# A streaming encoder layer on one core: full-width gate, sample and decay products, mLSTM's old part scaled on ScalarE, and a table of additions by tile name in the order pass

## The chip, the cores and the metric

The kernel runs on one core of one Trainium2 chip. The metric is the device time of one execution in microseconds (us), lower is better. TensorE (PE), VectorE (DVE), ScalarE (ACT), GpSimd (POOL) and SyncE (SP, which here issues the DMA transfers) each run one list of instructions in the order in which it was written and wait for each other with semaphores.

## What is computed

One layer of a streaming encoder, on 1024 new prompt frames (no history) and 32 frames of a running stream with state, model width 1024:

```python
h, st = mixer(rms_norm(x, g_mix_pre), st, ...)
x = x + rms_norm(h, g_mix_post)
h, ffn_buf = conv_ffn(rms_norm(x, g_ffn_pre), ...)
x = x + rms_norm(h, g_ffn_post)

def mixer(xn, ...):
    gq, gk, gv, gg, gr, hq, hf, hi, hg, mq, mk, mv, mi, mf, mo = split(xn @ w_in)
    # GLA: 6 heads 32x64, log_a = log_sigmoid(gg @ gla_w_gate + b) / 16   (gg has 16 columns)
    # HGRN2: 5 heads 64x64, gate from hf
    #   both: S_t = diag(a_t) S_{t-1} + k_t v_t^T, o_t = S_t^T q_t
    # mLSTM: 5 heads 64x64, gates mi and mf (5 columns each), causal conv on q and k
    #   m_i = max(g, max_j dlog);  w = exp(dlog - m_i);  w0 = exp(g - m_i)
    #   num = (s * w) @ v + w0 * (q @ C);   den = sum(s * w) + w0 * (q @ n)
    cat = concat(head_norm(o) * gate(o) for the three groups)
    return cat @ w_out, states

def conv_ffn(xn, ...):
    gate, val = split(causal_dwconv(xn @ w_up, width 3))   # 2 x 2816 columns
    return (gelu(gate) * val) @ w_down
```

All is float32. The states and the last rows of the convolutions are outputs too.

## The kernel before, in words

**Precision.** A product of float32 matrices runs as three passes over high and low halves (`mm3`, lines 88 to 91; `split` makes the halves: a cast on ScalarE, line 95, and a subtraction, line 98). Names with h and l at the end are these halves, with r the raw weights.

**Units and groups.** The 1056 frames are nine units u: eight of 128 prompt frames and u = 8 with the 32 sample frames (DEC). Three groups g of units are projected together: 384, 384 and 256 + 32 columns. `xh`, `xl` hold a group's normalized frames by features (line 309 transposes, 311 and 312 split).

**Projection in.** Features-by-frames products `pf` (13 blocks, `feat`) feed q, k and gates. Frames-by-features products give the values v and output gates: for groups 0 and 1 `vg(blk)` (line 420) makes them directly in `pv`, for each unit with its own `xh` columns as the fixed operand; so for u = 8 that operand is 32 columns wide. Group 2 runs blocks 1 to 7 in `vg_across` (line 432): products `pv` by features for all 288 columns, ScalarE copies them to `vf` (line 450), and `back` transposes each unit into `pb` (line 438). `vg_store` (line 403) passes a result on (ScalarE copy, or a tanh and a VectorE product) and stores it to `v_d` and `g_d`. A weight's raw half is loaded at line 321; in groups 1 and 2 its low half comes back from `lt_d` (line 325), where group 0 stored it.

**Gates.** Block 0 also holds 26 gate columns (16 for GLA, 5 and 5 for mLSTM). They are copied to `tgs` (line 428), and three small products a unit with the identity (line 473) bring them onto partitions 64 to 79, 96 to 100 and 32 to 36 of `tg`; ScalarE copies them to `r_fm` and `r_ig` (474 to 476). `z0` and `z3` (529, 604) are GLA's gate products from the 16 rows; `rows` (533) scans mLSTM's gates, spreads chunk decays by `dcp` (582) and transposes per-frame scales into `cols` (588, tile of the `mi` ring).

**Mixer.** `mixer(u)` (line 674) works through chunks with many small products (32 or 64 rows and columns): transposed keys `kt` and `kw` (762 to 802), state updates `up`, outputs `og` and `oh` (line 776), scores by levels, `oi` (queries by old mLSTM state) and `om`. Lines 936 to 940 join mLSTM's parts: `hn` is `oi` times w0 from `cols` (two VectorE products over 3 and 2 heads of 65 columns), then `om` is added. `sd` (960) are the diagonal scores. It runs beside the projections of later groups.

**The rest.** `outproj` (1009), FFN up with seven block products `puw` to `puz` of a fast matrix multiplication (1145 to 1310), down likewise (`down_all`, 1312; `wd` its weights). `T1h`, `B22h` and such are halves of sums of blocks.

**What sets the order.** `order` (line 2013) takes the finished program, builds a graph of dependencies with a cost for each instruction, and simulates all five engines (`play`): each takes, of what is ready in the simulation, the instruction with the largest priority. The result is fixed as the order of each engine. The priority is the longest path to the end in ns, plus an addition from the table `AHEAD`: the first key with which the name of the instruction's first output tile begins counts, otherwise the key of its pool.

```python
name.startswith(k)), pool))                                     # 1808: first key of AHEAD, or the pool
return [t + AHEAD.get(p, 0) for t, p in zip(tail, self.pool)]   # 1856
```

For TensorE `choose` stays in a tile mode while it can, and leaves full products for small ones only where the small work collected is `GATE` ns or more or has waited `PATIENCE` ns, and its priority is `CHANGE` ns ahead.

## Time and profile before

| | |
|---|---|
| three runs | 1331.88, 1327.99, 1328.19 us; median 1328.19 |
| profiled execution, its time | 1327.83 us |
| its span in the trace | 1326.0 us |
| mean granted TensorE clock | 0.993 |
| first matrix product / end of the last | 1.75 / 1318.3 us |
| FFN up and most of down | 645 to 1130 us |

One execution was profiled. The page lists busy time by engine and by group of instructions; the trace also answers by stretch of time, by wait and as a timeline. A group reads: line, engine, operation, output <- inputs, shapes, xcount, busy us, mean ns, idle before. In a wait, the engine and line that waited stand left of the arrow, what ended the wait right of it. A timeline row has start, duration, engine, line, operation, xcount and, in brackets, the idle time before it and what released it. `128*16` is a tile mode: rows and columns of the array that the fixed operand takes. Matrix products are pipelined, so that a product's duration is longer than the distance between two starts.

### The profile page before, as it was taken

The numbers are of one execution on the slowest core, as the hardware profiler recorded it, in microseconds if no ns is written. First come the engines' busy times: TensorE is split into PE (matmuls) and PEld (weight loads), VectorE is DVE, ScalarE is ACT, GpSimd is POOL, SyncE is SP. The second block draws the span as 40 slices with busy tenths as digits, with TensorE's granted clock in tenths as the row PEclk, the third lists the DMA queues.
The fourth block names the chain that finished last, engine by engine and source line by source line (L and its number), as shares of the span: only waits on it lengthen the run. The fifth ranks groups of instructions, "written<-read, shape, count | busy, mean of one in ns | idle before, by whom it ended". The sixth has DMA issues, their size and how long they took to land. (4 is left out here: it accounts for less than half of the span.)

```text
span 1326.0 us, 30530 instructions
## 1 busy us (share of the span) xinstructions
PE 1293.3 (98%) x12005; PEld 1208.7 (91%) x12005; DVE 1034.2 (78%) x1877; ACT 724.8 (55%) x1432; POOL 181.1 (14%) x331
## 2 busy tenths in 40 slices
PE   8999999999998999999999999999999999999997
PEld 7999999999898888778899999999999999888886
DVE  6795559748788478779899998888888878676686
ACT  6555566546576454436754545445454455365664
POOL 2020001111011112223112211111111110010010
PEclk9999999999999999999999999999999999999999
DMA  9899879977899863545256643222232268887774
GB/s 333 283 337 334 268 264 317 318 252 247 279 317 297 307 234 116 176 119 157 104 191 195 217 153 121 95 99 81 90 121 97 97 217 286 295 273 259 226 251 179
DMA packets 148455, 285.25 MB, mean 215 GB/s; under 512 B 30071, under 2 KB 84503, under 8 KB 148311
## 3 DMA queue, kind: packets, MB, share of 16 engines
q1 hardware_dynamic: 148311, 283.30, 63.7%
q8 instruction: 94, 1.54, 0.5%
q14 instruction: 50, 0.41, 0.1%
HBM read 201.90 MB, written 81.34 MB: 214 GB/s over the span
## 5 line engine op out<-in xcount | busy, mean ns | idle before, releaser
L1257 DVE SCALAR_TENSOR_TENSOR y<-uu,fconv_sb,y 128x1060 f32<-128x1060 f32 x88 | 116.0, 1321 | 7.7 <-ACT y L1255 6.7
L98 DVE TENSOR_TENSOR hlp<-rp,hhp 128x384 fp32r<-128x384 f32 x77 | 42.5, 555 | 35.3 <-PE pdw L91 11.3
L1255 ACT ACTIVATE y<-uu,fconv_sb 128x1060 f32<-128x1060 f32 x44 | 56.2, 1277 | 22.9 <-POOL uu L1252 17.1
L95 ACT CAST hhp<-rp 128x384 fp32r<-128x384 f32 x77 | 39.6, 515 | 49.0 <-PE pdx L90 18.2
L1203 ACT COPY c<-pux 128x274 f32<-128x274 f32 (+1 forms) x132 | 46.2, 380 | 27.1 <-PE pux L91 25.0
L933 POOL TENSOR_TENSOR hrs<-hss,mhalf 128x5 f32<-128x5 f32 (+3 forms) x27 | 36.1, 1340 | 163.8 <-DVE hss L932 162.8
L98 DVE TENSOR_TENSOR wdp<-rp,wdp 128x512 fp32r<-128x512 f32 x77 | 52.0, 688 | 3.7 <-ACT wdp L95 2.6
L89 PE MATMUL pv<-wt_0h,xh 128*128 128x256 f32 (+2 forms) x195 | 53.1, 294 | 1.4 <-ACT xh L311 0.6
L95 ACT CAST wdp<-rp 128x512 fp32r<-128x512 f32 x77 | 47.0, 621 | 10.1 <-PE pdx L91 3.4
L91 PE MATMUL pv<-wt_0h,xl 128*128 128x256 f32 (+2 forms) x195 | 50.6, 286 | 0.2 <-DVE xl L312 0.2
L90 PE MATMUL pv<-wt_0l,xh 128*128 128x256 f32 (+2 forms) x195 | 50.4, 284 | 0.2 <-DVE wt_0l L98 0.2
L91 PE MATMUL pv<-wt_1h,xl 128*128 128x256 f32 (+2 forms) x195 | 48.1, 287 | 0.0
L89 PE MATMUL pv<-wt_1h,xh 128*128 128x256 f32 (+2 forms) x195 | 47.2, 285 | 0.0
L90 PE MATMUL pv<-wt_1l,xh 128*128 128x256 f32 (+2 forms) x195 | 46.9, 285 | 0.0
L1252 POOL COPY uu<-fcache_sb 128x2 f32<-128x2 f32 x44 | 19.0, 431 | 185.8 <-DVE uu L1208 185.8
L91 PE MATMUL pdx<-wdp,hlp 128*128 128x512 f32 x132 | 43.2, 391 | 0.0
L90 PE MATMUL pdx<-wdp,hhp 128*128 128x512 f32 x132 | 43.0, 389 | 0.0
L89 PE MATMUL pdx<-wdp,hhp 128*128 128x512 f32 x132 | 42.7, 391 | 0.0
L1254 POOL COPY fhalo<-uu 128x2 f32<-128x2 f32 x44 | 35.7, 812 | 50.5 <-DVE uu L1208 49.9
L89 PEld LDWEIGHTS pv<-wt_0h,xh 128*128 128x128 f32 (+1 forms) x195 | 34.8, 187 | 2.8 <-ACT xh L311 0.9
L211 POOL TENSOR_SCALAR gss<-gss 128x1 f32<-128x1 f32 (+1 forms) x9 | 6.7, 747 | 216.6 <-ACT gjk L1331 132.5
L91 PEld LDWEIGHTS pv<-wt_0h,xl 128*128 128x128 f32 (+1 forms) x195 | 34.3, 187 | 1.0 <-issue 0.4
(1784 smaller groups left out, 5124.4 us busy)
## 6 DMA issues: line engine op xcount, KB each, us to landing
h_d<-y SPq DMA_DIRECT2D x22, 530.0 KB, 3.3
rp<-t_d SPq DMA_DIRECT2D x44, 256.0 KB, 3.9
wt_0r<-in_w_tok SPq DMA_DIRECT2D x21, 512.0 KB, 6.1
wt_1r<-in_w_tok SPq DMA_DIRECT2D x21, 512.0 KB, 5.5
...
```

The source lines that it names most:

```text
L89: pe.matmul(ps, lh[0], rh[0], start=first, stop=False, **kw)
L90: pe.matmul(ps, lh[0], rh[1], start=False, stop=False, **kw)
L91: return pe.matmul(ps, lh[1], rh[0], start=False, stop=last, **kw)
L95: act.copy(hi, src)
L98: (eng or pool).tensor_tensor(lo, src, hi.bitcast(F32), op=ALU.subtract)
L211: pool.tensor_scalar(out, ss, other, EPS, op0=ALU.add, op1=ALU.add)
L933: pool.tensor_tensor(rs[:n, h0:h0 + nh], ss[:n, h0:h0 + nh], mhalf[:n, :nh], op=ALU.pow)
L1203: act.copy(t, ps)
L1252: pool.tensor_copy(u[:, GAP_S:GAP_S + 2], fcache[:, j, :])
L1254: pool.tensor_copy(fhalo[:, j, :], u[:, NCOL - 2:NCOL])
L1255: act.activation(y, u, AF.Identity, scale=fconv[:, j, 2:3], bias=fconv[:, j, 3:4])
L1257: dve.scalar_tensor_tensor(y, uu[i][:, s:s + NCOL], fconv[:, j, s:s + 1], y, op0=ALU.mult, op1=ALU.add)
```

## The change

The diff has four parts.

1. **Full rows and columns.** The sample unit's products and transposes (`pv`, `pb`, `kw`, `sd`, `turned`) use a 128-column operand that ends with its 32 frames, so results stand on partitions 96 to 127. `tgs` becomes a 128-column tile, zeroed on GpSimd, filled by a ScalarE copy of 16 columns and a VectorE copy of 2 x 5, and a unit's three products into `tg` become one full transpose. `z0` and `z3` read 96 rows instead of 16 (the others are zero in the weights), `z3` writes 128 columns; `dcp` reads 128 rows. For u = 8 four transposes and two copies to `kt` become one and four. The host swaps the mi and mf columns and moves a bias.
2. **hn on ScalarE.** Two VectorE products a unit become five ScalarE copies with a scale.
3. **The table.** `AHEAD` gets some 480 keys with values from -10500 to 18000 ns; most name single tiles. The key `pt` (130000) goes; many mixer tiles that went by their pool's 10000 have a key of their own.
4. `GATE` goes from 300 to 500 and `PATIENCE` from 3000 to 4000.

```diff
 def vg_store(blk, u, off, n, ps):
+    r = slice(128 - n, 128)
-        act.copy(o[:n], ps[:n, :256])
-        sp.dma_start(v_d[t:t + n, 256 * blk:256 * blk + 256], o[:n])
+        act.copy(o[r], ps[r, :256])
+        sp.dma_start(v_d[t:t + n, 256 * blk:256 * blk + 256], o[r])
...
 # vg
-    mm3(ps[:n, :N], (xh[:, k, off:off + n], xl[:, k, off:off + n]), ws[k], k == 0, k == 7)
+    mm3(ps, (xh[:, k, off + n - 128:off + n], xl[:, k, off + n - 128:off + n]), ws[k], k == 0, k == 7)
-    act.copy(tgs[:n, i, :], ps[:n, 256:])
+    act.copy(tgs[:, i, 64:80], ps[:, 256:272])
+    dve.tensor_copy(tgs[:, i].rearrange("p (a b) -> p a b", b=64)[:, :, 32:37],
+                    ps[:, 272:282].rearrange("p (a b) -> p a b", b=5))
 # back
-    pe.transpose(ps[:n, 128 * e:128 * e + 128], fs[e][:, off:off + n], ident)
+    pe.transpose(ps[:, 128 * e:128 * e + 128], fs[e][:, off + n - 128:off + n], ident)
 # gates
-tgs = pf.tile([128, 3, 26], F32, tag="tgs", name=f"tgs{g}")
+tgs = pf.tile([128, 3, 128], F32, tag="q", name=f"tgs{g}", bufs=2)
+pool.memset(tgs, 0.0)
-    for (r0, c0, c1) in ((64, 0, 16), (96, 16, 21), (32, 21, 26)):
-        pe.matmul(gt_[r0:r0 + c1 - c0, off:off + n], tgs[:n, i, c0:c1], ident[:n, :n], start=True, stop=True)
-act.copy(gg[64:80], gt_[64:80, :T])
+    pe.transpose(gt_[:, off + n - 128:off + n], tgs[:, i], ident)
+act.copy(gg[:96], gt_[:96, :T])
-pe.matmul(z0[:, :T], wg[64:80, 0:128], gg[64:80, :], start=True, stop=True)
+pe.matmul(z0[:, :T], wg[:96, 0:128], gg[:96], start=True, stop=True)
-pe.matmul(z3[:64, :T], wg[64:80, 128:192], gg[64:80, :], start=True, stop=True)
+pe.matmul(z3[:, :T], wg[:96, 64:192], gg[:96], start=True, stop=True)
...
 # rows
+pool.memset(dc, 0.0)
-    pe.matmul(dcp[:, f, :ci], self_[R, 128 * f:128 * f + 128], dc[R, :ci], start=True, stop=True)
+    pe.matmul(dcp[:, f, :ci], self_[:, 128 * f:128 * f + 128], dc[:, :ci], start=True, stop=True)
-    pe.transpose(pt[:n, :], st[:, off:off + n], ident)
+    pe.transpose(pt, st[:, off + n - 128:off + n], ident)
...
 # mixer
+if u == 8:
+    kps = small(128)
+    pe.transpose(kps, khf, ident)
+    for f in range(4):
+        act.copy(kt[:n, 128 * f:128 * f + 128], kps[n * f:n * f + n])
-for f0 in (0, 2):
+for f0 in (0, 2) if u < 8 else ():
...
-for e in range(2):
-    dve.tensor_tensor(hn[:n, e::2], ois[e][:n, :3 - e],
-                      cols[:n, 32:37].unsqueeze(2)[:, e::2].broadcast_to([n, 3 - e, 65]), op=ALU.mult)
+for h in range(5):
+    act.activation(hn[:n, h], ois[h % 2][:n, h // 2], AF.Copy, scale=cols[:n, 32 + h:33 + h])
...
-AHEAD = {"mx": 10000., "psm": 10000., "pdx0": 1400., "pdx1": 700., "pdw0": 1400., "pdw1": 700., "pt": 130000.}
-GATE, PATIENCE = 300., 3000.
+AHEAD = {
+    "fconv_sb": 2000, "wt0_1_0r": -2500, "wt0_2_0l": 500, "wt0_2_1r": -1000, "wt0_3_0h": -1000, "wt0_3_0l": -3500, "wt0_4_0h":
...
+    500, "uu": -1500, "v2": 4000, "v4": 2500, "v6": 1000, "v7": -8000, "vf": 6000, "vg": -4000, "w2": 500, "wd": -9000, "wf":
...
+GATE, PATIENCE = 500.0, 4000.0
```

What it does to the order, on both built programs: TensorE issues 10081 products and transposes for 10102, and leaves full tiles for smaller ones 79 times for 106. Nearly every instruction moves by some places; three places follow. In the rows, `x2` and such count equal instructions in a row.

The first is TensorE in group 0, from the last gate product to `z0`. `pf_8` is the projection of block 8. Before:

```order
L89 MATMUL pf_8_376<-xh_185,wf_8h 128x384
L90 MATMUL pf_8_376<-xl_186,wf_8h 128x384
L91 MATMUL pf_8_376<-xh_185,wf_8l 128x384
L473 MATMUL tg_356<-ident,tgs_202 16x128
L473 MATMUL tg_356<-ident,tgs_202 5x128 x2
L529 MATMUL z_0_419<-r_fm_354,wg_sb 128x384
L89 MATMUL pf_6_433<-xh_185,wf_6h 128x384
```

With the change:

```order
L89 MATMUL pf_8_374<-xh_185,wf_8h 128x384
L476 MATMUL tg_360<-ident,tgs_202 128x128
L90 MATMUL pf_8_374<-xl_186,wf_8h 128x384
L91 MATMUL pf_8_374<-xh_185,wf_8l 128x384
...
L89 MATMUL pf_8_374<-xh_185,wf_8h 128x384
L90 MATMUL pf_8_374<-xl_186,wf_8h 128x384
L532 MATMUL z_0_417<-r_fm_358,wg_sb 128x384
L91 MATMUL pf_8_374<-xh_185,wf_8l 128x384
L89 MATMUL pf_6_431<-xh_185,wf_6h 128x384
```

`z_0` stood right behind the gate products and now stands 13 products of `pf_8` behind the gate transpose.

The second is TensorE in group 2, where the transposes of block 4 go back (`pb7_4`, `pb8_4`: units 7 and 8); `og5`, `oh5` are output products of unit 5, `sm80` and `sm81` scores of unit 8. Before:

```order
L91 MATMUL pv2_5_1_6621<-xh2_4321,wt2_5_1l_6583 128x288
L672 MATMUL mi_167<-ident_126,kh8_7017 32x128 x2
L438 MATMUL pb7_4_6647<-ident_126,vf4_6503 128x128 x2
L438 MATMUL pb8_4_6655<-ident_126,vf4_6503 32x128 x2
L776 MATMUL sm80_7027<-mqk8_6902 32x32 x3
L776 MATMUL sm81_7028<-mqk8_6902 32x32 x2
L89 MATMUL pv2_6_0_6676<-xh2_4321,wt2_6_0h_6665 128x288
```

With the change:

```order
L91 MATMUL pv2_5_1_6636<-xh2_4328,wt2_5_1l_6598 128x288
L785 MATMUL og5_5335<-v5_5077,P_184 64x64 x3
L785 MATMUL oh5_5336<-v5_5077,P_184 64x64
...
L785 MATMUL oh5_5336<-v5_5077,P_184 64x64
L592 MATMUL mi_167<-ident_126,r_st_2_5789 128x128
L441 MATMUL pb7_4_6662<-ident_126,vf4_6518 128x128 x2
L441 MATMUL pb8_4_6670<-ident_126,vf4_6518 128x128
L89 MATMUL pv2_6_0_6691<-xh2_4328,wt2_6_0h_6680 128x288
```

Twenty-two small products of unit 5, which stood further up, and a transpose now stand between block 5 and the transposes of block 4; the 32-row transposes of unit 8 are full ones, and its scores have gone elsewhere.

The third is SyncE in group 2, around the load of the second low half of block 2 (`wt2_2_1l`). Before:

```order
L325 DMA wt2_2_0l_6328<-lt_d_94 128x1024
L321 DMA wt2_3_1r_6414<-in_w_tok 128x1024
...
L373 DMA out_q_mc<-pc_2_6169 128x3
L321 DMA wt2_4_0r_6491<-in_w_tok 128x1024
L691 DMA v5_5064<-v_d_84 128x704
L325 DMA wt2_2_1l_6334<-lt_d_94 128x1024
L325 DMA wt2_3_0l_6411<-lt_d_94 128x1024
```

With the change:

```order
L325 DMA wt2_2_0l_6343<-lt_d_94 128x1024
L321 DMA wt2_3_1r_6429<-in_w_tok 128x1024
L373 DMA out_q_mc<-pc_2_6184 128x3
L374 DMA out_p_mc<-pc_2_6184 128x3
L325 DMA wt2_2_1l_6349<-lt_d_94 128x1024
L321 DMA wt2_4_0r_6506<-in_w_tok 128x1024
L325 DMA wt2_3_0l_6426<-lt_d_94 128x1024
L325 DMA wt2_3_1l_6432<-lt_d_94 128x1024
L695 DMA v5_5077<-v_d_84 128x704
```

The low half now stands ahead of the next raw weight and of unit 5's values; the store of a unit's result and loads of unit 5's keys and masks, which are not shown, stand further up than before. At the start of SyncE's list the gain row `gx` (512 KB) comes ahead of the first frames `x0`, which stood first.

More of the change, by code (lines that the diff above doesn't have):

```diff
@@ L411, in vg_store @@
             th = mx.tile([128, 256], F32, tag="vth", name=f"vth{u}_{blk}", bufs=1)
-            tanh(th[:n], ps[:n, :256], 0.5)
+            tanh(th[r], ps[r, :256], 0.5)
             ns = min(max(704 - c0, 0), 256)
             if ns:
-                dve.scalar_tensor_tensor(o[:n, :ns], th[:n, :ns], 1.0, ps[:n, :ns], op0=ALU.add, op1=ALU.mult)
+                dve.scalar_tensor_tensor(o[r, :ns], th[r, :ns], 1.0, ps[r, :ns], op0=ALU.add, op1=ALU.mult)
             if ns < 256:
-                dve.tensor_scalar(o[:n, ns:], th[:n, ns:], 1.0, None, op0=ALU.add)
-            sp.dma_start(g_d[t:t + n, c0:c0 + 256], o[:n])
+                dve.tensor_scalar(o[r, ns:], th[r, ns:], 1.0, None, op0=ALU.add)
+            sp.dma_start(g_d[t:t + n, c0:c0 + 256], o[r])
         def vg(blk):
@@ L587, in rows @@
                 pt = small(128)
-                pe.transpose(pt[:n, :], st[:, off:off + n], ident)
+                pe.transpose(pt, st[:, off + n - 128:off + n], ident)
                 cl = mx.tile([128, 128], F32, tag="cols", name=f"cols{u}", bufs=6)
-                act.copy(cl[:n], pt[:n])
+                act.copy(cl[:n], pt[128 - n:])
                 cols_of[u] = cl
@@ L603, in inproj @@
         z3 = psb.tile([128, 512], F32, tag="big", name=f"z3_{g}")
-        pe.matmul(z3[:64, :T], wg[64:80, 128:192], gg[64:80, :], start=True, stop=True)
+        pe.matmul(z3[:, :T], wg[:96, 64:192], gg[:96], start=True, stop=True)
         def fill3(fr):
-            act.activation(fr[:64], z3[:64, :T], AF.Identity, bias=vecs[:64, 3:4])
+            act.activation(fr[:64], z3[64:, :T], AF.Identity, bias=vecs[64:, 3:4])
             act.copy(fr[64:], ps3[64:, :T])
@@ L796, in mixer @@
             for f in range(2 if h0 == 0 else 1):
-                first(pe.transpose, kp[:n, 2 * f:2 * f + 2, :].rearrange("p h d -> p (h d)"),
-                      mk[:, f, :] if h0 == 0 else mq[:, 2, :], ident)
+                into = kp[:, 2 * f:2 * f + 2, :].rearrange("p h d -> p (h d)")
+                if u < 8:
+                    first(pe.transpose, into, mk[:, f, :] if h0 == 0 else mq[:, 2, :], ident)
+                else:
+                    first(pe.transpose, into, mqk[:, n * f:n * f + 128], ident)
+            kr = slice(0, 128) if u < 8 else slice(96, 128) if h0 == 0 else slice(64, 96)
             if h0:
                 kp = kp[:, 1:2]
-            dve.tensor_tensor(kw[:n, h0:h1], kp[:n, :h1 - h0],
+            dve.tensor_tensor(kw[:n, h0:h1], kp[kr, :h1 - h0],
                                        cols[:n, 96 + h0:96 + h1].unsqueeze(2).broadcast_to([n, h1 - h0, 64]), op=ALU.mult)
@@ L959, in mixer @@
         sd = small(11)
+        if u == 8:
+            dve.memset(z[:, 128:224], 0.0)
         for f in range(4):
-            first(pe.matmul, sd[:n], z[:, f * n:f * n + n], of_head[:, f, :], start=f == 0, stop=f == 3)
+            first(pe.matmul, sd, z[:, f * n:f * n + 128], of_head[:, f, :], start=f == 0, stop=f == 3)
         put(0, sd[:n].unsqueeze(2).broadcast_to([n, 11, cl]))
@@ L1404, in turned @@
                 for d in range(4):
-                    pe.transpose(pts[hf][:n, 128 * d:128 * d + 128], accs[4 * hf + d][:, off[u]:off[u] + n], ident)
+                    pe.transpose(pts[hf][:, 128 * d:128 * d + 128], accs[4 * hf + d][:, off[u]:off[u] + 128], ident)
             finish(u, n, [p[:n] for p in pts])
@@ L1605, in body @@
     p4s.close()
-CHANGE = 1500.
-BACKLOG = 2000.
-SLACK = {"PE": 1000.}
-AHEAD = {"mx": 10000., "psm": 10000., "pdx0": 1400., "pdx1": 700., "pdw0": 1400., "pdw1": 700., "pt": 130000.}
-GATE, PATIENCE = 300., 3000.
+CHANGE = 1500.0
+BACKLOG = 2000.0
+SLACK = {"PE": 1000.0}
+AHEAD = {
[58 rows of a table added]
+    2000, "jk4": 0, "jk5": 4000, "jk7": 2000, "lbt": 500, "oh7": -4000, "oml": 2000, "pdx": -2000, "psm": 10000, "pux": 500,
[8 rows of a table added]
+GATE, PATIENCE = 500.0, 4000.0
 ENGINES = ("PE", "DVE", "Activation", "Pool", "SP")
@@ L2038, in _layout @@
     w_tok = np.ascontiguousarray(wt[1:])
-    w_tok0 = np.hstack([wv[:, :256], gg, mf, mi]).reshape(8, 128, 282).transpose(1, 0, 2)
+    w_tok0 = np.hstack([wv[:, :256], gg, mi, mf]).reshape(8, 128, 282).transpose(1, 0, 2)
     w_out = np.asarray(i["w_out"])[0][of_plane].reshape(8, 128, 1024)
@@ L2046, in _layout @@
     vecs[:, 0] = bg[:128]
-    vecs[:64, 3] = bg[128:]
+    vecs[64:, 3] = bg[128:]
     lb = np.asarray(i["hgrn_lb"])[0]
```

64 rows, old and new, of the table AHEAD are left out of this document.

## The prediction

> **What bounds the kernel now.** I read the page's first part, then busy times by stage, the waits of TensorE, and the timelines around the waits that the change touches.
>
> ```profile
> span 1326.0 us, 30530 instructions
> PE 1293.3 (98%) x12005; PEld 1208.7 (91%) x12005; DVE 1034.2 (78%) x1877; ACT 724.8 (55%) x1432; POOL 181.1 (14%) x331
> ```
>
> TensorE is busy 98% of the span, so work on the other engines counts only where TensorE waits for it. The stage table says where it does (first column of each pair busy us, then count; the last three columns are granted clock, DMA share, GB/s).
>
> ```profile
> 0.00:50.00 50.00, 44.67 (x269) 40.74 (x270) 34.66 (x61) 27.64 (x50) 10.46 (x29) 1.00 0.92 329
> 300.00:400.00 100.00, 98.39 (x1545) 92.24 (x1544) 83.49 (x213) 67.18 (x152) 13.30 (x20) 0.98 0.86 282
> 400.00:500.00 100.00, 92.23 (x1097) 81.97 (x1096) 70.59 (x179) 55.35 (x134) 11.94 (x12) 0.98 0.83 275
> 500.00:600.00 100.00, 97.02 (x1267) 76.28 (x1267) 77.39 (x160) 47.03 (x112) 22.37 (x31) 0.98 0.47 142
> 600.00:645.00 45.00, 40.87 (x237) 35.42 (x236) 37.60 (x43) 32.45 (x67) 11.39 (x13) 0.97 0.40 122
> 645.00:1130.00 485.00, 485.00 (x3915) 485.00 (x3915) 422.70 (x641) 243.11 (x433) 74.94 (x176) 1.00 0.42 147
> 1130.00:1160.00 30.00, 28.33 (x192) 26.01 (x191) 21.66 (x39) 12.81 (x26) 0.00 (x0) 1.00 0.90 297
> ```
>
> From 645 to 1130 (the FFN) TensorE never stops at full clock: a new order can win nothing there, only lose. Idle TensorE time is 5.3 us in the first stage, 1.6, 7.8, 3.0 and 4.1 in the four from 300 to 645, 1.7 around 1145: 23.5 in all. The first stage's 5.3 is mostly the first loads. Four waits that bear on the change, from the list of TensorE's waits (us in total, times, longest):
>
> ```profile
> PE pv L91 <- DMA wt_1l<-lt_d: 1.8, 1, 1.8
> PE puw L89 <- ACT T1h L1133: 1.5, 1, 1.5
> PE pb L438 <- ACT vf L450: 1.0, 1, 1.0
> PE z L529 <- ACT r_fm L474: 0.7, 1, 0.7
> ```
>
> Beside waiting, TensorE loses time to a granted clock of half. Two of its four such stretches, each with the stretch ahead of it (the third number from the end is the clock):
>
> ```profile
> 448.20:451.60 3.40, 1.91 (x19) 1.35 (x20) 2.27 (x9) 3.15 (x9) 0.70 (x1) 1.00 0.94 307
> 451.60:455.00 3.40, 3.40 (x17) 3.38 (x16) 0.27 (x1) 0.00 (x0) 0.00 (x0) 0.50 1.02 387
> 536.90:540.30 3.40, 2.88 (x33) 2.50 (x33) 1.72 (x4) 3.34 (x10) 0.86 (x2) 1.00 0.62 176
> 540.30:543.70 3.40, 3.40 (x46) 2.61 (x41) 3.40 (x5) 1.97 (x6) 0.00 (x0) 0.50 0.13 17
> ```
>
> Each is 3.4 us long and costs half of it, 1.7 us; four cost 6.8. Both follow a stretch in which TensorE was not fully busy, but 2.88 of 3.40 was already too little.
>
> **(a) Fewer changes of tile mode.** In the built order TensorE switches between full products (128 rows and columns) and smaller tiles 149 times where it did 194 times, in 79 detours for 106. A detour of before, the gates of two units:
>
> ```profile
> 163.74 0.29 PE L91 MATMUL pv<-wt_2h,xl 128*128 128x282 f32 x1
> 163.96 0.61 PE L473 MATMUL tg<-ident,tgs 128*16 128x128 f32 x12
> 164.50 0.44 PE L89 MATMUL pf<-xh,wf_8h 128*128 128x384 f32 x1
> 164.78 0.33 PE L90 MATMUL pf<-xl,wf_8h 128*128 128x384 f32 x1
> 164.96 0.34 PE L91 MATMUL pf<-xh,wf_8l 128*128 128x384 f32 x1
> ```
>
> The start of tg comes 0.22 us after the product before it, where such products elsewhere in this stretch follow each other in 0.13; the product behind the detour holds the engine 0.28 us where the next holds it 0.18. So a switch costs about 0.1 us, and 45 fewer save 4.5. The bounds: −2 if more than half of the switches removed stood in time when TensorE waited anyway; −8 if what is narrow in the 27 detours is saved too (tg alone: 0.54 for a pair against two full transposes of at most 0.15 by the row further down, 0.1 a unit, 0.9 in nine units, and 0.1 more a detour for the rest).
>
> Widening the sample unit's products costs nothing in themselves:
>
> ```profile
> 326.24 0.30 PE L89 MATMUL pv<-wt_0h,xh 128*32 128x282 f32 x1
> 326.37 0.29 PE L90 MATMUL pv<-wt_0l,xh 128*32 128x282 f32 x1
> ```
>
> Products of 32 columns start 0.13 apart, as the full ones do. [...]
>
> **(b) The wait of z0, −0.7** (0 to −0.7). In group 0 of before, z0 comes right behind the last tg. Now 13 pf_8 products, 0.18 us each by the rows at 164.78 and 164.96, stand between them: 2.3 us over a wait of 0.7. The copy that z0 waits for reads 96 rows instead of 16, on partitions side by side, so it gets no longer.
>
> **(c) The low half of weight block 2, −0.9** (0 to −1.8).
>
> ```profile
> 400.26 0.38 SPq L321 DMA_DIRECT2D wt_0r<-in_w_tok  x1
> 401.25 0.32 SPq L691 DMA_DIRECT2D v<-v_d  x1
> 402.55 0.32 SPq L325 DMA_DIRECT2D wt_1l<-lt_d  x1
> 408.33 0.40 PE L91 MATMUL pv<-xh,wt_1l 128*128 128x288 f32 x1 [1.84 <-DMA wt_1l<-lt_d]
> ```
>
> The load is issued at 402.55 behind a weight (wt_0r) and a load of v, and its product waits 1.84. Now it stands ahead of both, 402.55 − 400.26 = 2.3 us earlier by these rows. But larger transfers (a 768 KB set of keys, masks, the store of a unit's result) now stand further up on the same queue, at a DMA share of 0.83: half of the wait is what I take.
>
> **(d) Transposes back in group 2, −1.9** (0 to −2.7).
>
> ```profile
> 447.31 1.03 ACT L327 CAST wt_0h<-wt_0r 128x1024 fp32r<-128x1024 f32 x1
> 448.24 0.38 ACT L450 COPY vf<-pv 128x288 f32<-128x288 f32 x1
> 448.68 0.44 PE L438 MATMUL pb<-ident,vf 128*128 128x128 f32 x2 [0.99 <-ACT vf L450]
> ```
>
> The copy vf stands behind a weight's cast of 1.03 us on ScalarE, and pb waits 0.99 for it. Now 22 small products of the mixer stand ahead of these transposes of block 4; they fill the wait: −1.0. The half-clock stretch from 451.6 has its cause here, in a stretch busy 1.91 of 3.40: filled by 1.0 it has 2.9, by the row at 536.9 still not surely enough, so half of its 1.7 is counted: −0.9. [...]
>
> **(e) The start, +1.0** (0 to +1.7).
>
> ```profile
> 0.72 0.40 SPq L144 DMA_DIRECT2D x<-in_xp  x1
> 1.17 0.42 SPq L155 DMA_DIRECT2D gx<-in_grows  x1
> 8.23 0.90 ACT L95 CAST wt_0h<-wt_0r 128x846 fp32r<-128x846 f32 x1 [2.33 <-DMA wt_0r<-in_w_tok]
> 9.67 0.40 PE L89 MATMUL pv<-wt_0h,xh 128*128 128x282 f32 x1 [0.64 <-ACT xh L311]
> ```
>
> The gain row gx (spread over 128 partitions, 512 KB) now is issued ahead of the first x. The chain to the first product at 9.67 goes from x by its norm and transposes to xh; x lands later by up to 512 KB at 329 GB/s = 1.6 us. The first weight only lands at 8.2, so part of it is hidden, but the first product waits for xh, not for the weight: +1.0.
>
> **(f) The FFN's start, 0.**
>
> ```profile
> 636.12 0.60 PE L1101 MATMUL fxt<-ident,z 128*128 128x128 f32 x4
> 638.75 1.23 DVE L1144 TENSOR_TENSOR xg<-xg 128x1024 f32<-128x1024 f32 x1
> 640.23 0.38 PE L89 MATMUL puw<-T1h,S_0h 128*128 128x256 f32 x1 [1.48 <-ACT T1h L1133]
> ```
>
> (Four transposes in 0.60 are the 0.15 used above.) T1h is cast ahead of B22h now, up to 1 us earlier; but its sum ends on VectorE at 639.98, and T1l and the next sums follow there at 1.2 us each, so the second product waits instead. Nothing is counted.
>
> **(g) mLSTM's old part on ScalarE, +0.5** (0 to +7.9).
>
> ```profile
> L938 DVE TENSOR_TENSOR hn<-oi,cols x18: 270/314/364, 171.9 to 570.4; 128x195 f32<-128x195 f32 x8, 128x130 f32<-128x130 f32 x8, 32x195 f32<-32x195 f32 x1, 32x130 f32<-32x130 f32 x1
> L1104 ACT ACTIVATE xg<-fxt,gcols_sb 128x128 f32<-128x128 f32 x24 | 7.2, 379 | 0.4 <-PE fxt L1101 0.4
> ```
>
> Two products of 0.314 on VectorE a unit (0.63) become five scaled copies. The nearest row, scaled copies of 128 columns out of PSUM, gives 7.2 / 24 = 0.30 each: 1.5, so hn comes up to 0.9 later, 7.9 in nine units. In the new order 14 to 113 TensorE products stand between the one that feeds hn and the next that needs its buffers, over 1.8 us at 0.13; only unit 8 has four. Half of one unit counts. VectorE gets 5.6 us back, which no TensorE wait of before asked for.
>
> The other edits cost 0: two more copies a unit into the gate tile, its three memsets and dc's on GpSimd (14% busy), and unit 8's two more ScalarE copies lie beside TensorE's products; if that cover is gone, each is 0.2 to 0.4 by the copy row at 448.24.
>
> **(h) All the rest of the order, −6.** The table moves nearly every instruction, and I can follow only a few places. What there is to win: 23.5 idle and 6.8 of half clock, 30.3, less 3.5 counted in (b), (c), (d): 26.8. At the places followed, waits of 5.0 us (z0, wt_1l, pb, puw) give back 2.6, and the start takes 1.0: net 1.6 of 5.0, a third. I take a quarter, since moved loads make new waits that no row shows: two loads for the down projection now stand behind more stores. Bounds: half of it, −13, and +8, the same waits growing by 30%.
>
> **Sum:** −4.5 −0.7 −0.9 −1.9 +1.0 +0 +0.5 −6 = −12.5. The profiled execution took 1327.83 (span 1326.0 and 1.8 around it), 0.36 below the median of 1328.19, so the two need no correction: 1315. Its own range, with (a) and (h) the widest terms, is 1306 to 1324.
>
> **The rivals.**
>
> *The order gives nothing (0.16).* Only (a), (e) and (g) hold, the waits come back elsewhere: −4.5 + 1.0 + 0.5 = −3.0, 1324.8. That is within 0.3% (4 us), about what a measurement of this kernel can tell from no change. For it: between 645 and 1130 nothing can be won. Against it: the waits of (b) and (d) visibly get cover.
>
> *The order gives far more (0.15).* If (h) takes 70% of the 26.8, −19: 1302. For it: the idle time lies in 300 to 645, where much small work is at hand to fill it. Against: (e) and (f).
>
> *ScalarE becomes the late engine (0.07).* If hn is waited for in every unit: −13.0 + 7.9 = −5.1, 1322.7. For it: in 448.2 to 451.6 ScalarE is busy 3.15 of 3.40. Against: 0.55 over the whole span.
>
> *Half clock spreads (0.11), the slower side.* The new settings gather small products longer (500 and 4000 ns for 300 and 3000) and release them in longer detours. At 536.9, 33 products, TensorE busy 2.88 of 3.40, and the clock halved for the next 3.4 us. If the longer detours of units 0 to 8 (130 to 600) each leave such a stretch, every one costs 1.7. Without (h) the sum is −6.5: four more stretches cancel it, from seven on it is slower by over 0.3%, and ten give −6.5 + 17 = +10.5, 1338. Against: fewer detours, and 100 to 300, full of small work, has clock 1.00.
>
> **How the numbers follow.** The forecast keeps 0.51. The range leaves out the tail of the large gain (under 1300) and that of the half clock (over 1331): 1300 to 1331. Faster by over 0.3%: forecast, large gain and late ScalarE, 0.51 + 0.15 + 0.07 = 0.73; the same: 0.16; slower: 0.11.
>
> **What would show it.** Right: tg's transposes without a gap of 0.1 around them, no wait of z0 and of pb for vf in the list of TensorE's waits, 400 to 500 with 94 or more busy, the first product near 10.7, puw still waiting about 1.5. Wrong: idle TensorE time between 645 and 1130, more than six stretches at clock 0.50, waits for hn or for a load of the down projection over 2 us, or a time over 1331 or under 1300.

## The result, and the profile after

| | before | with the change |
|---|---|---|
| runs, median | 1328.09 us (1324.92 to 1331.88, 4 runs) | 1311.62 us (1309.83 to 1314.21, 4 runs) |
| ratio | | 0.9875, 95% interval 0.9852 to 0.9899 |
| profiled execution, its time / span | 1327.83 / 1326.0 us | 1314.21 / 1312.4 us |

The change takes off 16.5 us by the medians and 13.6 by the profiled spans; the profiled execution of the changed kernel is the slowest of its four. 1315 was forecast, in a range of 1300 to 1331. A second measurement of the same kernel, among the experiments below, gave a ratio of 0.9897 (0.987 to 0.9924).

The page of the changed kernel begins so:

```profile
span 1312.4 us, 30429 instructions
PE 1285.7 (98%) x11957; PEld 1209.7 (92%) x11957; DVE 1024.5 (78%) x1869; ACT 728.5 (56%) x1479; POOL 169.6 (13%) x337
```

TensorE stands outside its busy time for 26.7 us of the span (1312.4 − 1285.7), where it was 32.7. The stages (same columns as before: stretch, busy us and count of TensorE, weight loads, VectorE, ScalarE, GpSimd, then granted clock, DMA share, GB/s):

```profile
0.00:50.00 50.00, 43.46 (x243) 41.74 (x244) 33.89 (x62) 27.21 (x49) 9.70 (x31) 0.93 0.93 323
100.00:200.00 100.00, 96.69 (x1043) 93.65 (x1042) 54.83 (x115) 55.49 (x112) 4.72 (x10) 1.00 0.85 295
300.00:400.00 100.00, 99.21 (x1591) 94.25 (x1591) 81.48 (x207) 67.83 (x162) 12.65 (x21) 1.00 0.86 289
400.00:500.00 100.00, 99.04 (x1272) 89.32 (x1272) 78.76 (x191) 65.45 (x162) 13.36 (x17) 1.00 0.83 287
500.00:600.00 100.00, 98.81 (x1184) 78.11 (x1183) 83.53 (x165) 52.08 (x130) 21.04 (x28) 1.00 0.48 151
600.00:645.00 45.00, 41.50 (x293) 38.36 (x292) 39.12 (x49) 32.16 (x63) 10.86 (x19) 1.00 0.37 125
645.00:1130.00 485.00, 483.92 (x3898) 483.46 (x3897) 410.45 (x636) 239.41 (x432) 68.17 (x168) 1.00 0.43 151
```

From 300 to 645 the idle time fell from 16.5 us to 6.4, and the clock is 1.00 throughout, where it was 0.97 to 0.98: 400 to 500, the worst stage of before, went from 92.23 busy to 99.04. The start got worse (5.3 idle to 6.5, clock 1.00 to 0.93). So did 100 to 200, which read in before:

```profile
100.00:200.00 100.00, 99.11 (x959) 94.85 (x959) 55.46 (x118) 56.53 (x111) 4.63 (x11) 1.00 0.85 288
```

The idle time there grew from 0.9 to 3.3 us; 1.2 of it is one wait of mi for kw, 1.3 one of pv for vg. From 645 to 1130, where TensorE never stopped before, it idles 1.1, in a wait of pd for hh; the second trace of the same kernel (experiment 5) has 485.00 busy there.

The longest waits of TensorE are mostly others now (us in total, times, longest; left out are one of 1.7 for the identity at the start, which both kernels have, and two of 1.0 and 0.8):

```profile
PE pv L89 <- ACT vg L408: 4.2, 4, 2.1
PE xt L309 <- DVE x L298: 2.6, 2, 1.6
PE pd L89 <- ACT wd L95: 1.8, 1, 1.8
PE mi L676 <- DVE kw L814: 1.2, 1, 1.2
PE puw L89 <- ACT T1h L1147: 0.8, 1, 0.8
```

The waits of pv for wt_1l (1.8), of pb for vf (1.0) and of z for r_fm (0.7) are gone from the list; puw waits 0.8 for 1.5. In their place stand pv for vg, the first transposes xt, and the last weight block wd of the first down stage. And the half-clock stretch at 451.6 is gone, with the emptier stretch ahead of it:

```profile
448.20:451.60 3.40, 3.40 (x28) 3.40 (x27) 3.37 (x15) 2.69 (x13) 1.16 (x1) 1.00 0.98 318
451.60:455.00 3.40, 3.40 (x60) 3.10 (x59) 3.21 (x10) 3.13 (x5) 0.00 (x0) 1.00 0.99 369
1137.20:1140.60 3.40, 1.63 (x13) 1.40 (x12) 0.75 (x2) 0.82 (x2) 0.00 (x0) 1.00 0.76 297
1140.70:1144.10 3.40, 3.40 (x16) 3.40 (x16) 2.71 (x6) 2.65 (x7) 0.00 (x0) 0.52 0.58 220
```

The third and fourth row are one of the three stretches that are left or new: the wait for wd leaves TensorE busy 1.63 of 3.40, and the next 3.4 us run at half clock. The other two lie in the first 30 us.

To see what kind of time went, I took from the traces the distance from each recorded product's start to the next, halved it where the clock was 0.50 (the half taken off is "half clock"), subtracted what such a product takes undisturbed in before (mean of the middle half), and sorted the rest: over 0.2 us is a wait, at a full product or in and beside a detour to small ones. Sums in us from the first start to the last:

| | before | changed | again | edits only | table only | kinds only | dealt out |
|---|---|---|---|---|---|---|---|
| products at their undisturbed pace | 1224.0 | 1222.5 | 1222.5 | 1222.7 | 1224.0 | 1222.0 | 1223.9 |
| surplus under 0.2, full products | 13.3 | 11.9 | 11.8 | 14.0 | 13.4 | 11.2 | 13.3 |
| surplus under 0.2, small products | 24.4 | 24.0 | 23.8 | 23.5 | 24.3 | 24.3 | 24.6 |
| surplus under 0.2, at a switch | 15.2 | 14.5 | 14.7 | 14.4 | 16.0 | 14.9 | 14.6 |
| waits at full products | 20.0 | 20.0 | 19.6 | 30.1 | 26.1 | 25.6 | 43.4 |
| waits in and beside detours | 12.4 | 5.5 | 4.1 | 4.6 | 9.8 | 6.8 | 12.8 |
| half clock | 6.8 | 5.1 | 3.4 | 1.7 | 12.0 | 6.8 | 18.8 |

("Again" is the second measurement, the other columns are experiments below.) The change wins 6.9 us of waits at detours, 1.7 of half clock, and 4.0 in the first four rows; the waits at full products are other ones, but as long as before. The two executions of the changed kernel differ by 3.6 us in sum, 1.7 of it half clock and 1.4 waits at detours, so differences of this size in one row say little. Of the 12.4 us of waits at detours in before, 2.1 (1.4 near 428 and 0.7 near 422, between small products) ended in nothing that the profile shows; why they are gone is not known. The other waits at detours of before all end with work of ScalarE or VectorE, so that little of them can be the hidden price of a switch.

### The profile page after: what moved, and what is told of

It is laid out like the page before. It is cut to its first block, busy times and chain, and to the rows that moved or that the text cites. A ratio compares the mean times of both kernels' runs of the same rounds, so it can differ in the third digit from the quotient of the medians.

```text
span 1312.4 us, 30429 instructions
## 1 busy us (share of the span) xinstructions
PE 1285.7 (98%) x11957; PEld 1209.7 (92%) x11957; DVE 1024.5 (78%) x1869; ACT 728.5 (56%) x1479; POOL 169.6 (13%) x337
## 4 chain that ended last, share of the span: by engine, by line
PE 84%; DMA 7%; ACT 4%; DVE 3%; issue 1%; SPq 1%; POOL 0%; DVEq 0%; POOLq 0%; ACTq 0%
PE pux L91 5%; PE pux L90 5%; PE pux L89 5%; PE pv L89 4%; PE pv L90 4%; PE pv L91 4%; PE pf L89 4%; PE pf L90 3%; PE pf L91 3%; PE puw L90 3%; PE puw L89 3%; PE puw L91 3%; PE zp L89 3%; PE zp L91 2%; PE zp L90 2%; PE pdx L89 2%
## 5 line engine op out<-in xcount | busy, mean ns | idle before, releaser
L1269 ACT ACTIVATE y<-uu,fconv_sb 128x1060 f32<-128x1060 f32 x44 | 56.0, 1275 | 11.7 <-DVE uu L1222 8.9
L89 PE MATMUL pv<-wt_0h,xh 128*128 128x256 f32 (+1 forms) x195 | 55.4, 296 | 3.8 <-ACT vg L408 3.8
L91 PE MATMUL pv<-wt_0h,xl 128*128 128x256 f32 (+1 forms) x195 | 53.8, 288 | 0.0
L90 PE MATMUL pv<-wt_0l,xh 128*128 128x256 f32 (+1 forms) x195 | 53.7, 287 | 0.0
L89 PE MATMUL pv<-wt_1h,xh 128*128 128x256 f32 (+1 forms) x195 | 51.1, 287 | 0.0
L91 PE MATMUL pv<-wt_1h,xl 128*128 128x256 f32 (+1 forms) x195 | 51.0, 288 | 0.0
L90 PE MATMUL pv<-wt_1l,xh 128*128 128x256 f32 (+1 forms) x195 | 50.9, 288 | 0.0
L1265 POOL COPY uu<-uu 128x2 f32<-128x2 f32 x44 | 24.0, 545 | 166.9 <-DVE uu L1222 166.7
L89 PEld LDWEIGHTS pv<-wt_0h,xh 128*128 128x128 f32 x195 | 36.2, 191 | 5.1 <-ACT vg L408 4.4
L90 PEld LDWEIGHTS pv<-wt_0l,xh 128*128 128x128 f32 x195 | 36.4, 191 | 0.0
L91 PEld LDWEIGHTS pv<-wt_0h,xl 128*128 128x128 f32 x195 | 36.3, 191 | 0.1
```

The costliest lines, as they stand in the source:

```text
L89: pe.matmul(ps, lh[0], rh[0], start=first, stop=False, **kw)
L90: pe.matmul(ps, lh[0], rh[1], start=False, stop=False, **kw)
L91: return pe.matmul(ps, lh[1], rh[0], start=False, stop=last, **kw)
L1265: pool.tensor_copy(u[:, GAP_P:GAP_P + 2], u[:, GAP_S - 2:GAP_S])
L1269: act.activation(y, u, AF.Identity, scale=fconv[:, j, 2:3], bias=fconv[:, j, 3:4])
```

## The experiments

They were run in three groups on three chips, each in five rounds beside the kernel before on the same chip; the ratio is to it, and between groups the ratios are compared. The first question is which part of the change makes the gain.

**1. The edits alone.** In the changed kernel:

```diff
-AHEAD = {"fconv_sb": 2000, ...}
-GATE, PATIENCE = 500.0, 4000.0
+AHEAD = {"mx": 10000., "psm": 10000., "pdx0": 1400., "pdx1": 700., "pdw0": 1400., "pdw1": 700., "pt": 130000.}
+GATE, PATIENCE = 300., 3000.
```

> The changed code with the old table and the old GATE and PATIENCE. Tile modes change 152 times (149 with the whole change, 194 before). Theory (switches 0.1 us each, the order for the rest): 42 fewer switches give -4.2 and hn +0.5, so about 1324 us against 1328 before, with +-4 for the waits that any new order brings. Rival A (the edits are the gain, the table only shifts waits): 1311 to 1314. Rival B (a switch costs nothing because TensorE waits there anyway): 1328.

Measured: 1322.01 us, 0.997 (0.9951 to 0.9988). The size is what the theory asked for, but not for its reason. By the table above, the 42 switches fewer take off 0.8 us, not 4.2. Waits at detours fall by 7.8 and the half clock by 5.1, and 10.1 us of new waits at full products take most of it back. Among them are these two, 0.3 and 0.7 in before; the wait of puw for T1h is 1.5 as before, and only the whole change has it shorter (0.8):

```profile
PE pv L89 <- DVE xl L312: 1.4, 1, 1.4
PE z L532 <- ACT r_fm L477: 1.2, 1, 1.2
```

**2. The table alone.** In the kernel before, the opposite exchange.

> The old code with the new table, GATE and PATIENCE. Tile modes change 187 times. Theory: -0.7 for 7 switches fewer, and the order's part without the edits, about -10 by what the changed kernel shows: 1316 to 1320 us. Rival A (the edits are the gain): 1326 to 1330. Rival C (the table fits only the program for which its numbers were made, and its keys meet other costs here): 1324 or more.

Measured: 1338.24 us, 1.0104 (1.0081 to 1.0127). The table makes the old code slower by 1%, so Rival C holds: it does not carry a gain of its own. The loss is waits at full products (+6.1) and half clock (+5.2), which comes three times for 6.8 us on end (from 10.4, 344.9 and 399.5); the last of them:

```profile
396.10:399.50 3.40, 1.00 (x6) 0.57 (x4) 2.81 (x6) 3.38 (x9) 0.25 (x1) 1.00 0.94 314
399.50:402.90 3.40, 2.35 (x8) 2.00 (x9) 2.90 (x7) 1.99 (x6) 0.55 (x1) 0.50 1.03 401
402.90:406.30 3.40, 3.40 (x37) 3.04 (x37) 3.23 (x11) 2.18 (x6) 1.36 (x2) 0.50 0.89 293
```

A stretch busy 1.00 of 3.40 is followed by one at half clock that itself is busy only 2.35, and then by another. The edits by themselves give −4.6, the table by itself +11.7, both together −16.5 (−14.7 in the second measurement): they do not add.

**3. The same numbers on other keys.** The changed kernel, the table's values dealt out anew at random:

```diff
-AHEAD = {"fconv_sb": 2000, "wt0_1_0r": -2500, "wt0_2_0l": 500, ...}
+AHEAD = {the same keys; the same values in random order; mx, psm, pdx0, pdx1 and t as they were}
```

> The changed kernel with the numbers of the table dealt out at random to the same keys (mx, psm and the four pd keys keep theirs), so that the keys, GATE and PATIENCE stay and only the fit of the numbers goes. Theory (each number is worth what its place gives): the order's part is lost, 1322 to 1330 us. Rival D (the freer keys and the longer gathering of small products make the gain, whatever the numbers): 1309 to 1315.

Measured: 1364.19 us, 1.0286 (1.0259 to 1.0314). Far over what the theory gave: this wrong table, one draw, costs 42 us over the edits alone, in waits for operands and in half clock (18.8 us, 11 stretches). The longest wait:

```profile
PE xt L309 <- DVE x L298: 5.5, 1, 5.5
```

**4. Kinds of tiles only.** The table has 537 keys (not some 480). Here is the changed kernel with 72 of them, the 70 without a digit and pdx0 and pdx1:

```diff
-AHEAD = {"fconv_sb": 2000, "wt0_1_0r": -2500, "wt0_2_0l": 500, ...}
+AHEAD = {k: v for the keys without a digit, and pdx0, pdx1}
```

> The changed kernel with only those keys of the table that hold no digit (72: whole kinds of tiles such as wd, hlp, vg, t) beside pdx0 and pdx1; the 465 keys for single tiles go. Theory (the numbers fit single places of one order, and half of the table is another order): no better than the old table, 1320 to 1335 us. Rival (the gain is in the kinds, single tiles are trimming): 1311 to 1316.

Measured: 1325.12 us, 0.9991 (0.9972 to 1.0009). The theory holds: without the keys of single tiles the gain is gone, and the kinds alone are no better than the old table. That the single keys would carry it without the kinds was not run. Here wd, the latest load of the first down stage, is waited for almost twice as long as in the changed kernel; in before and in experiment 1 the wait is 0.4:

```profile
PE pd L89 <- ACT wd L95: 3.3, 1, 3.3
```

**5. The changed kernel again.** No edit.

> The changed kernel once more, beside the other three on the same chip: a ratio of 0.9875 within 0.002, and the same waits at the same places (first projection product at 11.9 us, pd for wd 1.8 us).

Measured: 1312.28 us, 0.9897 (0.987 to 0.9924), a little further from 0.9875 than the 0.002 expected. The same order gives the same waits, but they vary in length: the first product at 12.43, pd for wd 1.5, and pv for vg 2.5 us in total in place of 4.2. Its profiled execution had two half-clock stretches, the first one's three, and the two spans (1308.4 and 1312.4) are 4.0 us apart: one profiled execution is good to no more than that.

The next question is whether the new waits can be had back.

**6. The first frames ahead of the gain row, by the table.**

```diff
-"gx": 4000,
+"gx": 1000,
```

> The changed kernel with the key gx at 1000 in place of 4000: on SyncE the first frames are issued ahead of the gain row again, as before. Theory (the start's loss is the late x0, and the half-clock stretch after it comes from the emptier first 10 us): first projection product at 9.7 to 10.2 us in place of 11.9, no clock of 0.50 near 12, time 1308 to 1310 us. Rival E (the loads of the first 50 us set the pace there, at a DMA share of 0.93, and take the gain back): 1311 to 1313.

Measured: 1313.5 us, 0.991 (0.989 to 0.993). The first product came at 9.86 and no microsecond of it reached the end. But the experiment doesn't decide, since the one key changed the simulated times from the first microsecond on, and with them rows of TensorE's order all along: between the end of the projections (463.6 here, 461.9 with the change) and the end of the output products (614.5 and 607.6) it lost 5 us, 3.4 of it to half clock from 485.5 and from 574.2. So the next ones fix the order: the pass of the changed kernel is run, and a few rows are exchanged in its result.

**7. The same exchange by hand, all else fixed.**

```diff
 seq = play(g, g.tails(), CHANGE, SLACK)[2]
+q = seq["SP"]
+q[0], q[1] = q[1], q[0]                      # x0, then gx
```

> The changed kernel with one exchange made by hand behind the order pass: on SyncE the first frames and the gain row change places, and every other row of every engine stays. Theory (the start's 2.2 us are lost for good because TensorE is behind by them until the end): first projection product near 9.9 us, time 1.5 to 2.5 us under the changed kernel, about 1309.5 where that takes 1311.6. Rival E (the stretch to 50 us is set by the loads, DMA share 0.93, and takes the gain back): time within 0.5 us of the changed kernel.

Measured: 1312.87 us, 0.9896 (0.9875 to 0.9916), as without it. And the first product came at 11.26, not 9.9. VectorE and TensorE in this run:

```profile
6.67 0.75 DVE L298 SCALAR_TENSOR_TENSOR x<-x,rs,gx 128x512 f32<-128x512 f32 x1 [2.72 <-POOL rs L212]
9.09 1.04 DVE L98 TENSOR_TENSOR wt_0l<-wt_0r,wt_0h 128x846 fp32r<-128x846 f32 x1 [1.67 <-ACT wt_0h L95]
10.04 0.74 DVE L298 SCALAR_TENSOR_TENSOR x<-x,rs,gx 128x512 f32<-128x512 f32 x1
```

```profile
10.85 0.66 PE L309 MATMUL xt<-ident,x 128*128 128x128 f32 x4 [2.71 <-DVE x L298]
```

The second half of the first x stands behind the first weight's low half in VectorE's order, and that waits for the weight to land. In before both halves of x came first. The change moved this row too.

**8. The first rows of three engines as before.** To 7:

```diff
+for e, k in (("DVE", 11), ("Activation", 2)):
+    seq[e][k], seq[e][k + 1] = seq[e][k + 1], seq[e][k]     # x ahead of wt_0l; xh ahead of jk1
```

> The changed kernel with three exchanges by hand behind the order pass, so that the first rows stand as before the change: x ahead of gx on SyncE, the second half of the first x ahead of the first weight's low half on VectorE, the first xh ahead of the second unit's squares on ScalarE. Theory (swap_gx won nothing since the second half of x still waited behind the weight): first projection product at 9.7 to 10.0 us, 1.5 to 2 us under the changed kernel. Rival E (the loads up to 50 us take it back): product at 9.8, time unchanged within 0.7 us.

Measured: 1313.34 us, 0.991 (0.9889 to 0.9931): Rival E. The first product is where it was before, and by 24 us nothing of it is left:

```profile
9.91 0.39 PE L89 MATMUL pv<-wt_0h,xh 128*128 128x282 f32 x1 [1.05 <-ACT xh L311]
24.21 0.60 PE L89 MATMUL pv<-wt_0h,xh 128*128 128x282 f32 x1 [2.50 <-ACT vg L408]
```

What takes it back is the wait of pv for vg, and the half clock behind it:

```profile
20.40:23.80 3.40, 1.31 (x11) 1.07 (x9) 2.24 (x8) 2.05 (x6) 0.78 (x2) 1.00 1.02 354
23.80:27.20 3.40, 2.99 (x13) 2.99 (x14) 1.14 (x2) 0.40 (x2) 0.00 (x0) 0.55 1.03 418
```

And behind that wait stands a load after all. In the same run:

```profile
20.24 1.06 ACT L294 ACTIVATE jk<-x 128x1024 bf16<-128x1024 f32 x1 [0.75 <-DMA x<-in_xp]
22.39 1.28 DVE L298 SCALAR_TENSOR_TENSOR x<-x,rs,gx 128x1024 f32<-128x1024 f32 x1 [1.05 <-POOL rs L212]
```

ScalarE waits for the frames of a later unit, VectorE's normalization for the scale that comes of them, and the copies on which pv waits stand behind that normalization (experiment 9 shows the rows). So the load and the order of these copies make the wait together, and Rival E is not refuted.

**9. The gate copies on ScalarE.** That wait is the change's own. In the changed kernel, around 23 us:

```profile
21.79 1.28 DVE L298 SCALAR_TENSOR_TENSOR x<-x,rs,gx 128x1024 f32<-128x1024 f32 x1 [0.66 <-POOL rs L212]
22.99 0.16 DVE L430 COPY tgs<-pv 128x10 f32<-128x10 f32 x1
23.19 0.37 ACT L408 COPY vg<-pv 128x256 f32<-128x256 f32 x1 [1.05 <-DVE tgs L430]
23.61 0.40 PE L89 MATMUL pv<-wt_0h,xh 128*128 128x282 f32 x1 [2.09 <-ACT vg L408]
```

The new copy of ten gate columns (L430, 0.16 us) stands on VectorE behind the normalization of a later unit; ScalarE's copy of the same PSUM tile waits for it, and the next pv for the tile. So, with the order of every engine taken over from the changed kernel:

```diff
-dve.tensor_copy(tgs[:, i].rearrange("p (a b) -> p a b", b=64)[:, :, 32:37],
+act.copy(tgs[:, i].rearrange("p (a b) -> p a b", b=64)[:, :, 32:37],
```

> The changed kernel with its order of every engine fixed; only the nine small copies of the ten mLSTM gate columns run on ScalarE, right behind the copy of the sixteen, in place of VectorE. Theory (the VectorE copy stands behind other work, the ScalarE copy vg of the same PSUM tile waits for it, and the next pv waits for that tile: 2.1 us in group 0 and 1.5 in group 1): the wait of pv for vg falls from 4.2 us to about 1, time 2 to 3 us under the changed kernel, ratio near 0.9875 where that has 0.9897. Rival (the next pv then waits for the low half xl of its own columns, as tg did before): waits of the same length with another name, no change within 1 us.

Measured: 1311.79 us, 0.99 (0.9875 to 0.9926): no change. The wait of pv for vg is shorter,

```profile
PE pv L89 <- ACT vg L408: 2.1, 4, 0.9
```

but experiment 5 had only 2.5 without the edit, with a longest wait of 1.7. So most of that fall may be a difference between executions. The profiled execution, the slowest of the six, had four half-clock stretches, two more than experiment 5's.

**10. The last weight ahead of the first down loads.** Near 1133 the changed kernel issues wd_21r late, behind loads of rp, and it takes 6.3 us to be used:

```profile
1133.43 0.40 SPq L1393 DMA_DIRECT2D wd_21r<-in_w_dn  x1
```

```profile
1139.78 1.14 ACT L95 CAST wd<-wd_21r 128x512 fp32r<-128x512 f32 x2 [3.79 <-DMA wd_21r<-in_w_dn]
1140.45 0.40 PE L89 MATMUL pd<-hh,wd 128*128 128x288 f32 x1 [1.77 <-ACT wd L95]
```

To 7:

```diff
+i, j = positions of the loads of wd0_20r and wd0_21r in q
+late = [rows between them that load rp1_]
+q[i:j + 1] = [n for n in q[i:j + 1] if n not in late] + late
```

> The kernel of swap_gx with a second change by hand: three loads for the first down product (rp1) stand behind the load of the last weight block wd0_21r, not ahead of it. Theory (the late weight costs 1.8 us of wait and 1.7 of half clock): the wait of pd for wd falls from 1.8 to under 1, the clock of 0.50 near 1142 goes, 2 to 3.5 us under swap_gx, about 1307. Rival (the block lands 5 to 6 us after its issue because its transfer shares the engines with the same loads, so that a place in the queue changes little; or rp1 is now the late one): 0 to -0.5 us, or slower.

Measured: 1310.59 us, 0.9879 (0.9859 to 0.9899). The wait of pd for wd fell to 0.2, from 2.3 in 7 and 1.5 in 5; it is 0.3 in experiment 11, which has the same exchange, and 1.5 to 2.1 in 8, 9 and 12, which have not. No stretch near 1142 runs at half clock. So the wait itself is mended. The time is 2.3 us under 7, on the side of the theory, but the two intervals overlap: not settled.

**11. All three mends.** 8, 9 and 10 in one fixed order.

> All three mends in the fixed order: the gate copies on ScalarE (tgs_act), the first rows as before (start_fix), and the rp1 loads behind the last weight block (swap_wd). If they add up: -2.5, -1.7 and -1.8, so 1306 us where the changed kernel takes 1312, ratio 0.985. If each only moves the wait to the next late load: 1309 to 1312.

Measured: 1311.28 us, 0.9891 (0.9867 to 0.9914). They do not add up; the start (product at 9.76) now runs into half clock at once:

```profile
10.20:13.60 3.40, 2.85 (x12) 2.31 (x13) 2.64 (x4) 3.22 (x6) 0.79 (x2) 0.73 0.99 355
13.60:17.00 3.40, 3.32 (x14) 2.63 (x14) 3.31 (x6) 1.57 (x4) 1.11 (x2) 0.50 0.94 285
```

No version was found that is clearly faster than the changed kernel.

**12. hn back on VectorE.** The order of every engine fixed as in the changed kernel, the two products right ahead of the addition:

```diff
-for h in range(5):
-    act.activation(hn[:n, h], ois[h % 2][:n, h // 2], AF.Copy, scale=cols[:n, 32 + h:33 + h])
+for e in range(2):
+    dve.tensor_tensor(hn[:n, e::2], ois[e][:n, :3 - e],
+                      cols[:n, 32:37].unsqueeze(2)[:, e::2].broadcast_to([n, 3 - e, 65]), op=ALU.mult)
```

> The changed kernel with its order of every engine fixed; only mLSTM's old part is scaled by two VectorE products a unit again, placed right ahead of the addition, in place of five ScalarE copies. Theory (TensorE waits for neither, VectorE is as late as ScalarE): within 1.5 us of the changed kernel, either way. Rival (the copies on ScalarE are on the path, 0.9 us in each of nine units): 5 us or more faster. Rival F (VectorE's 5.6 us are what the change won): 3 us or more slower.

Measured: 1318.76 us, 0.9946 (0.9925 to 0.9968): 6.5 us over experiment 5, as Rival F had it in size. The place is unit 8. The changed kernel (experiment 5's trace), ScalarE and then TensorE:

```profile
463.55 0.50 ACT L951 ACTIVATE hn<-oi,cols 32x65 f32<-32x65 f32 x2
464.03 0.24 PE L785 MATMUL oh<-S,qb 64*32 64x64 f32 x1
```

With hn on VectorE:

```profile
464.08 1.27 DVE L1020 SCALAR_TENSOR_TENSOR wo4l<-wor,hcol,wo4h 128x1024 fp32r<-128x1024 f32 x1
465.86 0.55 DVE L951 TENSOR_TENSOR hn<-oi,cols 32x195 f32<-32x195 f32 x2
466.27 0.30 PE L785 MATMUL oh<-S,qb 64*32 64x64 f32 x2 [0.88 <-DVE hn L951]
```

oh takes a PSUM buffer that oi holds until hn has read it. On VectorE, hn stands behind a weight's low half of 1.27 us and two short steps of vg (left out); TensorE waits 0.88, and then runs at half clock for 6.8 us on end, from 467.2 to 474.0:

```profile
465.40:468.80 3.40, 2.53 (x27) 2.30 (x28) 3.33 (x14) 0.77 (x2) 0.00 (x0) 0.76 0.62 200
468.80:472.20 3.40, 3.40 (x31) 3.03 (x29) 1.30 (x3) 3.05 (x4) 0.11 (x1) 0.50 0.64 149
```

From the last pv to the first product of the output projection it is 9.6 us (462.60 to 472.22) for 6.3 in experiment 5 (461.31 to 467.59): 3.3 more, and the half clock lasts beyond. TensorE's order is the same in experiments 5 and 7 to 12, so that starts of the same products can be set beside each other: from 463 to 470 of experiment 5 this run falls 4.1 us behind it. The two profiled spans are 8.5 apart. Of the rest, 1.5 is a half-clock stretch from 535.5, and some 2 are lost in the first down stage, where pd waits for hh twice (1.3); the first trace of the changed kernel has such a wait too. So about 4 us belong to this place. Since the order was made for copies on ScalarE, and the two products were put right ahead of the addition by hand, the size holds for this order only. Kernel 12 does not say what VectorE would cost in an order made for it.

## Why the prediction was right, and where it was not

The time, the sign and the likeliest case were right. That the sum lands so near is in part luck: by the table above, the switches gave 0.7 where 4.5 was forecast, the products' own pace 3.3 that was not in the sum, the half clock 1.7 for 0.9, and the waits 6.9 for 7.6. By its own steps:

- **(a) The price of a switch was wrong.** 0.1 us at each of 45 gave −4.5. The traces give 15.2 us for 182 recorded switches of before, 0.08 each, but 14.5 for 144 with the change, 0.10 each: the switches that went were those that cost next to nothing, 0.7 us in all (0.5 and 0.8 in the traces of experiments 5 and 1). The step that failed is the one that took a single detour's ends, which stood between full products at full pace, for the average of those removed. The bound −2 had the reason (switches in time in which TensorE waits anyway). With what narrow and full products themselves save, −4.0 came off, near the term but by another way. The widening itself cost nothing, as the row of 0.13 said: with the change the sample unit's products of 128 columns start 0.13 apart too, from 327.82 on. By these figures a switch costs 0.08 to 0.10 us on the average, and fewer of them need not be worth that.
- **(b), (d) held, and more than in full.** In the first trace no product waits for r_fm, and none over 0.3 for vf; the cover was there, and the copy of 96 rows takes 480 ns for 470 of the 16 rows. The wait for vf is not gone for good: in experiment 5 a pv near 444 waits 1.1 for it. The half clock at 451.6 went whole (1.7 for 0.9).
- **(c) held in full**, 1.8 for 0.9: the load came early enough in spite of the larger transfers ahead (issued at 398.82 for 402.55, its first product at 406.60).
- **(e) was too small, and no matter.** The first product came 2.2 us later, over the bound of 1.7, because I looked at SyncE's rows alone and not at VectorE's, where the second half of x had gone behind a weight (experiments 7 and 8). That it changes nothing at the end (8) was not foreseen: pv's wait for vg, with the load of a later unit's frames behind it, takes up what the start leaves.
- **(f)** The wait of puw fell by 0.7, and the second product still waits 0.6, as said; the half-clock stretch behind (1.7) went with it, which was not counted.
- **(g) is not borne out, and its sign is open.** +0.5 was forecast, with a bound that left a gain out, since "no TensorE wait of before asked for" VectorE's time. The copies take 10.7 us of ScalarE for 45,

```profile
L951 ACT ACTIVATE hn<-oi,cols 128x65 f32<-128x65 f32 (+1 forms) x45 | 10.7, 315 | 8.3 <-PE oi L785 8.1
```

  0.24 each, near the 0.30 taken; no product waits for them. In this order, VectorE would be the late engine at the very unit, 8, that was named as without cover, and would lose about 4 us there. No run has VectorE's products in an order made for them.
- **The gate copies were priced at nothing, and they are part of a new wait**: a copy of 0.16 us on another engine ordered two readers of one PSUM tile, and pv waits 2.5 to 4.2 us in total for vg in the two traces of the changed kernel. That this costs time is not shown: experiment 9 moved the copies, and neither the total wait (2.1) nor the time fell by more than executions differ.
- **(h) had the right size.** Waits fell by 6.9 on the whole, where (b), (c), the 1.0 of (d), (e) and (h) made −7.6, and the gains came from detours, not from the waits between full products that the list of waits shows best. The share was a guess (a quarter of 26.8 is 6.7, and 6 was taken), so the size is in part luck.
- **The rivals.** "The order gives nothing" fell with experiments 1 and 4: with the order of old, or of half the table, it is 1322 to 1325. "Half clock spreads" did not come true in the change (three stretches for four), but the two wrong orders brought it: 12.0 and 18.8 us of it in experiments 2 and 3. My break-even there counted stretches one by one; they come in pairs too: in experiment 2 three times, for 6.8 us each.
- **The signs.** 400 to 500 (99.04 busy), the two waits that go and the transposes of tg (one starts 0.13 us after the product ahead of it, at 23.98) came as said; the first product (11.9 for 10.7) and the wait of puw (0.8 for 1.5) did not. One sign of being wrong came: TensorE idles 1.1 us between 645 and 1130 in the first trace, and not in the second.

Up to the last product, half clock lasted 3.40 to 3.42 us at a time, or 6.82 to 6.83 on end, in before, in the changed kernel and in experiments 1 to 9, 11 and 12. At the end of before the clock is halved from 1322.0, 3.7 us after the last product (1318.3). Elsewhere half clock followed stretches busy 1.00 (experiment 2), 1.31 (8), 1.63 (the changed kernel), 2.53 (12) and, before, 2.88 of 3.40. It even followed a full one. In experiment 8, and then at the same products in experiment 5:

```profile
566.80:570.20 3.40, 3.40 (x64) 3.09 (x63) 3.28 (x9) 2.19 (x6) 1.18 (x2) 1.00 0.14 55
570.20:573.60 3.40, 3.40 (x9) 2.60 (x8) 3.17 (x6) 0.72 (x1) 2.08 (x1) 0.51 0.00 0
```

```profile
564.80:568.20 3.40, 3.40 (x65) 3.06 (x63) 3.31 (x7) 2.12 (x6) 1.19 (x2) 1.00 0.14 53
568.20:571.60 3.40, 3.40 (x17) 2.78 (x16) 3.12 (x6) 0.76 (x1) 2.13 (x1) 1.00 0.02 7
```

Small products and transposes in the same order fill both first stretches, and only one is followed by half clock (in experiments 6 and 9 it is, too, from 574.2 and 570.3). So the busy time that the profile shows does not tell which stretch will be.

What stays open: which of the 465 single keys carry the gain; what takes back the mends of 9 and 11, where waits and half clock at other places differ as much as between two executions of one kernel; and what the full-width products and hn win each, since no run has one without the other in an order of its own.
